# Splitting the weights of an fp32r encoder by two DMAs and a negation instead of a load, a cast and a subtraction

## The chip, the cores and the metric

The kernel runs on one core of one Trainium2 chip. The metric is the device time of one execution in microseconds, lower being better. The kernel before takes 1576.11 us (median of two runs, 1575.96 and 1576.26).

The core has five engines with a queue each, worked in order: TensorE (PE in the profile; PEld is its loading of the stationary operand), VectorE (DVE), ScalarE (ACT), GpSimd (POOL) and SyncE (SP). Transfers are started from a queue (SP or POOL here) and carried out by 16 DMA engines that all queues share.

## The reference

Two encoder layers over 512 positions of 1024 features, all in float32. Cut to the matrix products, which are nearly all of the work:

```
h = rmsnorm(x, g_mix[i]);  z = h @ w_in[i]              # 1024 -> 416 + 3*512 + 2*1024 columns
q = rmsnorm(c_q) @ w_uq[i];  kv = rmsnorm(c_kv) @ w_ukv[i]
...                                                     # per-head norm, rotary, softmax attention over 8 heads
y_conv = cb * dwconv(cc * cx, w_conv[i])
merged = g_a * (y_attn @ w_attn_up[i]) + g_c * (y_conv @ w_conv_up[i])
x = x + merged @ w_o[i]
u = dwconv(rmsnorm(x, g_ffn[i]) @ w_up[i], w_ffn_conv[i])   # 1024 -> 2 * 2816
x = x + (silu(a) * val) @ w_down[i]
x = x + sigmoid(rmsnorm(x, g_ple[i]) @ w_ple_gate[i]) * (p[i] @ w_ple[i])
```

## The kernel before

TensorE multiplies in float32r, a rounded form of float32. To keep precision each operand is held as two tiles: `h`, the operand rounded to float32r, and `lo`, the operand minus `h`. A product is then three matmuls (`mm3`, lines 88 to 90): h by h, h by lo and lo by h. A weight tile is 128 partitions by 1024 columns, 512 KB (416 KB for `w_a1`), and 250 of them go through the helper `weight` (line 78): 88 of `w_up`, 44 of `w_down`, 32 of `w_g`, 24 of `w_z`, 16 each of `w_o` and `w_pg`, 8 each of `w_au`, `w_cu` and `w_a1`, 4 of `w_ple` and 2 of `w_ukv`. `split` (line 92) does the same to activations, and to `w_uq` and `p`; it is not touched.

`weight` loads the tile from HBM into `raw` (three buffers) from SP's queue (line 80), casts it to `wh` on ACT (line 83) and subtracts on DVE to get `wl` (line 84). `wh` and `wl` have five buffers each. So up to three tiles can lie ready in `raw` while all five pairs are held by matmuls.

Two shapes of use matter. In `ws` (line 258) a weight is stationary: its 8 pieces by three matmuls, 24 in all, use it up before the next one (`w_z`, `w_g`, `w_up`; 4 pieces at a time for `w_au` and `w_cu`). In `proj` (line 511; `w_o`, `w_down`, `w_ple`, `w_pg`) the weights of one half of the output columns, four at a time with 8 input blocks, are all read again for each of the four blocks of 128 positions. They are therefore all held until the last block, and become free one after the other, shortly before those of the other half are wanted. This place is called a turn below.

A layer goes: latents with `w_a1`, heads, attention with the convolution's `w_z` products as filling work (here PE's order is written by hand), gates (`w_g`, `w_au`, `w_cu`), `w_o`, then three chunks of `w_up` and `w_down`, then `w_ple` and `w_pg`. Elsewhere a scheduler that simulates the kernel decides the order on every engine and which buffer a tile takes; a change of operations therefore also changes the order on PE. POOL does the small work of the norms (`rsqrt_eps`, lines 98 and 99) and of the rotary embedding (lines 242 to 253).

Of the kernel before, what the change touches and what calls it, by code (L numbers as in the profile page):

```python
# [11 lines left out]
F32 = mybir.dt.float32  # L12
# [3 lines left out]
AF = mybir.ActivationFunctionType  # L16
ALU = mybir.AluOpType
AX = mybir.AxisListType

P = 128  # L20
# [38 lines left out]
def encoder_kernel(ctx, tc, x_in, pT, pos, inv, w_a1, w_z, w_g, w_uq, w_ukv, w_au, w_cu, w_o,  # L59
                   w_up, w_down, w_pg, w_ple, b_gate, g_norm, g_lat, g_nope, g_rope, w_conv,  # L60
                   w_fconv, out):
    nc = tc.nc
    cp = ctx.enter_context(tc.tile_pool(name="cp", bufs=1))
    wp = ctx.enter_context(tc.tile_pool(name="wp", bufs=5))
# [11 lines left out]
        return ps.tile([P, S], F32, tag=tag, name="ps_" + tag, bufs={"mm": 2, "av": 1, "sc": 2, "tp": 3}[tag])  # L76

    def weight(src, n=1024):
        raw = wp.tile([P, n], F32, tag="raw", name="raw", bufs=3)
        nc.sync.dma_start(raw, src)  # L80
        h = wp.tile([P, n], F32R, tag="wh", name="wh")
        lo = wp.tile([P, n], F32R, tag="wl", name="wl")
        nc.scalar.copy(h, raw)  # L83
        nc.vector.tensor_sub(lo, raw, h.bitcast(F32))  # L84
        return h, lo

    def mm3(o, st, mv, start, stop):
# [100 lines left out]
    def layer(l, first):  # L188
        wa = []
        if first:  # L190
            nrm, close_nrm = pool("nrm", l)
            g1 = load_gain(l, 0, nrm)
            for i in range(4):
                wa.append(weight(w_a1[l, i], 2 * A1))
                if i < 3:
                    load_x(i + 1)
                norm(i, g1, nrm)
            close_nrm()
        else:
            wa = [weight(w_a1[l, i], 2 * A1) for i in range(4)]  # L200
# [6 lines left out]
        for i in range(2):  # L207
# [3 lines left out]
            split(w[0], w[1], raw)  # L211
            wu.append(w)
        wkv = weight(w_ukv[l])
        grope = mix.tile([P, 2, DR], F32, name="grope")
        nc.sync.dma_start(grope, g_rope[l:l + 1].broadcast_to([P, 2, DR]))
# [485 lines left out]
```

## Time and profile before

| | |
|---|---|
| median of the runs | 1576.11 us |
| span of the profiled execution | 1574.1 us |
| outside the span, against the median | 2.0 us |
| PE busy | 1557.1 us, 99% |
| DVE busy | 870.4 us, 55% |
| ACT busy | 684.4 us, 43% |
| POOL busy | 103.0 us, 7% |
| DMA from SP's queue | 140.90 MB, 27.2% of the 16 engines' time |
| granted TensorE clock, mean | 0.999 |

The profile is of one execution. Rows of operations give a line, an engine, the tile written and the tiles read, a count, the busy time in us and the mean in ns, and behind the bar the idle time of that engine just before, with what ended it. A busy time of PE is not PE at its peak, since matmuls overlap and their ends are modelled.

### The profile page before, as it was taken

How to read it: one execution, taken by the hardware profiler on the slowest of the kernel's cores; microseconds unless marked ns; L12 is line 12 of the kernel's file. 1: busy time of each engine (PE TensorE's matmuls, PEld its weight loads, DVE VectorE, ACT ScalarE, POOL GpSimd, SP SyncE). 2: the span in 40 equal slices, each digit the busy share in tenths (PEclk: the TensorE clock that was granted, in tenths of full speed). 3: DMA queues.
4: the chain of work that ended last, by engine and by line, in shares of the span. 5: the costliest groups of instructions: out<-in, count | busy, mean ns of one | idle time of the engine just before them, and what ended most of it. 6: DMA issues, size and time to landing. Idle time of an engine off the chain costs nothing.

```text
span 1574.1 us, 18521 instructions
## 1 busy us (share of the span) xinstructions
PE 1557.1 (99%) x7288; PEld 1280.1 (81%) x7288; DVE 870.4 (55%) x1228; ACT 684.4 (43%) x1088; POOL 103.0 (7%) x153
## 2 busy tenths in 40 slices
PE   7999999999999999999999999999999999999998
PEld 6888888888888888888888888888888888888886
DVE  7787553436544553555477775443565446535543
ACT  5678732325322431334464886222344234324342
POOL 2800000000000000001055000000000000000010
PEclk9999999999999999999999999999999999999999
DMA  6211122323213221323242102232232222232222
GB/s 205 93 55 41 54 94 94 106 69 129 95 61 130 93 95 58 132 96 94 71 133 81 41 28 92 81 107 81 85 118 94 94 94 94 80 107 94 94 68 79
DMA packets 41430, 142.06 MB, mean 90 GB/s; under 512 B 5761, under 2 KB 6273, under 8 KB 41345
## 3 DMA queue, kind: packets, MB, share of 16 engines
q1 hardware_dynamic: 41344, 140.90, 27.2%
q8 instruction: 57, 0.93, 0.2%
q14 instruction: 29, 0.23, 0.0%
HBM read 138.78 MB, written 2.10 MB: 90 GB/s over the span
## 4 chain that ended last, share of the span: by engine, by line
PE 94%; POOL 2%; DVE 2%; ACT 1%; DMA 1%; issue 1%; SPq 0%; DVEq 0%; POOLq 0%; ACTq 0%
PE ps_mm L89 14%; PE ps_mm L88 14%; PE ps_mm L90 14%; PE ps_sc L89 11%; PE ps_sc L88 11%; PE ps_sc L90 11%; PE ps_tp L89 4%; PE ps_tp L88 4%; PE ps_tp L90 4%; PE ps_tp L428 2%; PE ps_tp L125 1%; POOL rs L99 1%; PE ps_av L440 1%; PE ps_av L439 1%; PE ps_tp L394 1%; PE ps_av L88 1%
## 5 line engine op out<-in xcount | busy, mean ns | idle before, releaser
L84 DVE TENSOR_TENSOR wl<-raw,wh 128x1024 fp32r<-128x1024 f32 (+1 forms) x250 | 304.0, 1217 | 325.1 <-ACT wh L83 322.7
L83 ACT CAST wh<-raw 128x1024 fp32r<-128x1024 f32 (+1 forms) x250 | 260.8, 1046 | 425.6 <-PE ps_tp L90 120.3
L88 PE MATMUL ps_mm<-hh,wh 128*128 128x512 f32 (+1 forms) x832 | 326.4, 392 | 0.5 <-DVE ycv L355 0.5
L89 PE MATMUL ps_mm<-hl,wh 128*128 128x512 f32 (+1 forms) x832 | 322.9, 388 | 0.0
L90 PE MATMUL ps_mm<-hh,wl 128*128 128x512 f32 (+1 forms) x832 | 322.5, 388 | 0.0
L90 PEld LDWEIGHTS ps_mm<-hh,wl 128*128 128x128 f32 x832 | 156.6, 188 | 34.7
L88 PEld LDWEIGHTS ps_mm<-hh,wh 128*128 128x128 f32 x832 | 156.7, 188 | 33.2 <-DVE ycv L355 1.0
L89 PEld LDWEIGHTS ps_mm<-hl,wh 128*128 128x128 f32 x832 | 156.9, 189 | 32.5 <-DVE hl L94 0.4
L89 PE MATMUL ps_sc<-hl,wh 128*128 128x512 f32 (+1 forms) x368 | 142.2, 386 | 0.0
L90 PE MATMUL ps_sc<-hh,wl 128*128 128x512 f32 (+1 forms) x368 | 142.2, 386 | 0.0
L88 PE MATMUL ps_sc<-hh,wh 128*128 128x512 f32 (+1 forms) x368 | 142.1, 386 | 0.0
L98 POOL TENSOR_SCALAR ms<-ms 128x1 f32<-128x1 f32 (+2 forms) x40 | 15.8, 394 | 1389.0 <-ACT junk L117 1360.0
L89 PE MATMUL ps_tp<-wl,gth 128*128 128x512 f32 x256 | 100.6, 396 | 0.0
L90 PE MATMUL ps_tp<-wh,gtl 128*128 128x512 f32 x256 | 100.6, 395 | 0.0
L88 PE MATMUL ps_tp<-wh,gth 128*128 128x512 f32 x256 | 99.9, 395 | 0.0
L88 PEld LDWEIGHTS ps_sc<-hh,wh 128*128 128x128 f32 x368 | 69.3, 188 | 15.3
L90 PEld LDWEIGHTS ps_sc<-hh,wl 128*128 128x128 f32 x368 | 69.3, 188 | 15.3
L89 PEld LDWEIGHTS ps_sc<-hl,wh 128*128 128x128 f32 x368 | 69.3, 188 | 15.3
L93 ACT CAST gth<-fa 128x512 fp32r<-128x512 f32 x44 | 27.3, 620 | 120.1 <-DVE fa L574 120.1
L525 DVE TENSOR_TENSOR xs<-xs,ps_tp 128x512 f32<-128x512 f32 x32 | 21.6, 685 | 85.0 <-PE ps_tp L90 85.0
L572 ACT ACTIVATE fa<-fa 128x512 f32<-128x512 f32 x44 | 27.8, 632 | 88.5 <-DVE fa L547 88.5
L88 PEld LDWEIGHTS ps_tp<-wh,gth 128*128 128x128 f32 x256 | 48.1, 188 | 11.6
(242 smaller groups left out, 2671.2 us busy)
## 6 DMA issues: line engine op xcount, KB each, us to landing
raw<-in_w_up_dram SPq DMA_DIRECT2D x88, 512.0 KB, 3.5
raw<-in_w_down_dram SPq DMA_DIRECT2D x44, 512.0 KB, 3.4
raw<-in_w_g_dram SPq DMA_DIRECT2D x32, 512.0 KB, 3.5
raw<-in_w_z_dram SPq DMA_DIRECT2D x24, 512.0 KB, 3.5
raw<-in_w_o_dram SPq DMA_DIRECT2D x16, 512.0 KB, 3.5
raw<-in_w_pg_dram SPq DMA_DIRECT2D x16, 512.0 KB, 4.2
raw<-in_w_au_dram SPq DMA_DIRECT2D x8, 512.0 KB, 3.5
raw<-in_w_cu_dram SPq DMA_DIRECT2D x8, 512.0 KB, 3.5
```

The lines of the kernel that those rows point to most:

```text
L83: nc.scalar.copy(h, raw)
L84: nc.vector.tensor_sub(lo, raw, h.bitcast(F32))
L88: nc.tensor.matmul(o, st[0], mv[0], start=start, stop=False)
L89: nc.tensor.matmul(o, st[0], mv[1], start=False, stop=False)
L90: nc.tensor.matmul(o, st[1], mv[0], start=False, stop=stop)
L93: nc.scalar.copy(hi, src)
L98: nc.gpsimd.tensor_scalar_add(ms, ms, EPS)
L99: nc.gpsimd.tensor_tensor(r, ms, negh[:, :n], ALU.pow)
L125: nc.tensor.transpose(tp[:, j * P:(j + 1) * P], ht[:, j * P:(j + 1) * P], ident)
L428: nc.tensor.transpose(tp[:, k * P:(k + 1) * P], pe[:, k * P:(k + 1) * P], ident)
L525: nc.vector.tensor_tensor(xs[:, t, c], xs[:, t, c], o, ALU.add)
L572: nc.scalar.activation(a, a, AF.Silu)
```

## The change

`weight` no longer has a `raw` tile. A DMA from POOL's queue loads the tile straight into `wh`, converting to float32r on the way. ACT writes the negative of `wh` into `wl`. A second DMA from POOL's queue reads the same weights from HBM again and adds them into `wl`, which then holds the weight minus `wh`. Nothing else in the text is changed; the tiles `raw` of `w_uq` and `p` stay, and their loads stay on SP's queue.

```
     def weight(src, n=1024):
-        raw = wp.tile([P, n], F32, tag="raw", name="raw", bufs=3)
-        nc.sync.dma_start(raw, src)
         h = wp.tile([P, n], F32R, tag="wh", name="wh")
         lo = wp.tile([P, n], F32R, tag="wl", name="wl")
-        nc.scalar.copy(h, raw)
-        nc.vector.tensor_sub(lo, raw, h.bitcast(F32))
+        nc.gpsimd.dma_start(h, src)
+        nc.scalar.activation(lo, h.bitcast(F32), AF.Copy, scale=-1.0)
+        nc.gpsimd.dma_start(lo, src, accum_op=ALU.add)
         return h, lo
```

The scheduler makes a new order of this. Line numbers of the changed kernel are one lower from here on (its line 81 is the converting load, 82 the negation, 83 the adding DMA; 87 to 89 are the matmuls of `mm3`). Three places follow; the numbers in names only tell tiles of one program apart.

In the first run of `w_up` weights of the first layer, SP's queue had these loads in a row:

```order
L80 DMA raw_3672<-in_w_up_dram 128x1024
L80 DMA raw_3708<-in_w_up_dram 128x1024
L80 DMA raw_3748<-in_w_up_dram 128x1024
L80 DMA raw_3784<-in_w_up_dram 128x1024
L80 DMA raw_3822<-in_w_up_dram 128x1024
```

At that place POOL's queue now has loads (`wh`) and adding DMAs (`wl`, one number higher than its `wh`):

```order
L81 DMA wh_3650<-in_w_up_dram 128x1024
L83 DMA wl_3651<-in_w_up_dram 128x1024
L81 DMA wh_3689<-in_w_up_dram 128x1024
L81 DMA wh_3724<-in_w_up_dram 128x1024
L83 DMA wl_3690<-in_w_up_dram 128x1024
L83 DMA wl_3725<-in_w_up_dram 128x1024
L81 DMA wh_3761<-in_w_up_dram 128x1024
L83 DMA wl_3762<-in_w_up_dram 128x1024
L81 DMA wh_3796<-in_w_up_dram 128x1024
```

Nothing stood between the loads before. Now an adding DMA, which has to wait for the negation of its own `wh`, stands ahead of the next load: in turns behind one load and behind two.

At the turn of the first `w_down` chunk of the first layer (`wh_4102`, `wl_4103` and `wh_4108`, `wl_4109` are the first two weights of the other half, `gth` and `gtl` the split activation), PE's queue had:

```order
L88 MATMUL ps_tp_4124<-wh_4108,gth_3594 128x512
L88 MATMUL ps_tp_4150<-wh_4102,gth_3475 128x512
L89 MATMUL ps_tp_4150<-wl_4103,gth_3475 128x512
L90 MATMUL ps_tp_4150<-wh_4102,gtl_3476 128x512
L88 MATMUL ps_tp_4150<-wh_4102,gth_3475 128x512
L89 MATMUL ps_tp_4150<-wl_4103,gth_3475 128x512
L89 MATMUL ps_tp_4124<-wl_4109,gth_3594 128x512
L90 MATMUL ps_tp_4124<-wh_4108,gtl_3595 128x512
```

The same place now (`wh_4031` and `wh_4036` are the first two weights of the other half, `wh_4155` a weight of the next `w_up` run):

```order
L88 MATMUL ps_tp_4103<-wl_4032,gth_3423 128x512
L89 MATMUL ps_tp_4103<-wh_4031,gtl_3424 128x512
L87 MATMUL ps_tp_4103<-wh_4036,gth_3539 128x512
L87 MATMUL ps_mm_4160<-hh_71,wh_4155 128x512
L88 MATMUL ps_mm_4160<-hl_72,wh_4155 128x512
L88 MATMUL ps_tp_4051<-wl_4037,gth_3539 128x512
L89 MATMUL ps_tp_4051<-wh_4036,gtl_3540 128x512
```

The first matmul that needs the second weight's `lo` has moved back: 41 matmuls now stand between it and the last one that reads the buffer's old `wh`, where 30 stood before. Work of a third block of positions and of the next `w_up` run is put in between.

In the heads of the first layer POOL had these norms and rotary products in a row (`rs` is an inverse root, `ms` its argument):

```order
L98 TENSOR_SCALAR ms3_489<-ms3_489 128x3
L99 TENSOR_TENSOR rs3_493<-ms3_489,negh_74 128x3
L242 TENSOR_TENSOR sg_252<-sinT_82,grope_241 128x4x16 x4
L98 TENSOR_SCALAR ms24_549<-ms24_549 128x24
L251 TENSOR_TENSOR rb_510<-krope_261,sg_252 128x32
L99 TENSOR_TENSOR rs24_552<-ms24_549,negh_74 128x24
```

There it now has:

```order
L97 TENSOR_SCALAR ms3_484<-ms3_484 128x3
L83 DMA wl_624<-in_w_z_dram 128x1024
L98 TENSOR_TENSOR rs3_488<-ms3_484,negh_74 128x3
L83 DMA wl_720<-in_w_z_dram 128x1024
...
L97 TENSOR_SCALAR ms24_544<-ms24_544 128x24
L83 DMA wl_843<-in_w_z_dram 128x1024
L98 TENSOR_TENSOR rs24_547<-ms24_544,negh_74 128x24
L81 DMA wh_874<-in_w_z_dram 128x1024
```

The DMAs of the `w_z` weights have come in between the norms that the heads wait for.

## The prediction

> **What bounds the kernel now.** I read the page's busy times and chain first, then the costliest groups, then the waits, and last the timeline at a turn.
>
> ```profile
> span 1574.1 us, 18521 instructions
> PE 1557.1 (99%) x7288; PEld 1280.1 (81%) x7288; DVE 870.4 (55%) x1228; ACT 684.4 (43%) x1088; POOL 103.0 (7%) x153
> ...
> PE 94%; POOL 2%; DVE 2%; ACT 1%; DMA 1%; issue 1%; SPq 0%; DVEq 0%; POOLq 0%; ACTq 0%
> ```
>
> TensorE is the bound: it is busy 99% of the span and carries 94% of the chain that ended last. All that is not PE is 1574.1 - 1557.1 = 17 us, or 1.1%. No change that leaves the matmuls alone can gain 2%, and this one leaves them alone. The question is what it can lose.
>
> The pace of the matmuls is read from the timeline of PE in a `w_g` product:
>
> ```profile
> 300.42 0.39 PE L90 MATMUL ps_mm<-hh,wl 128*128 128x512 f32 x1
> 300.65 0.39 PE L88 MATMUL ps_mm<-hh,wh 128*128 128x512 f32 x1
> 300.88 0.40 PE L89 MATMUL ps_mm<-hl,wh 128*128 128x512 f32 x1
> 301.12 0.40 PE L90 MATMUL ps_mm<-hh,wl 128*128 128x512 f32 x1
> ```
>
> Three start in 0.70 us, so one takes 0.234 us, and the 24 of one weight tile 5.6 us. A new split tile has to be ready every 5.6 us wherever weights are streamed. How does it get ready?
>
> ```profile
> L84 DVE TENSOR_TENSOR wl<-raw,wh 128x1024 fp32r<-128x1024 f32 (+1 forms) x250 | 304.0, 1217 | 325.1 <-ACT wh L83 322.7
> L83 ACT CAST wh<-raw 128x1024 fp32r<-128x1024 f32 (+1 forms) x250 | 260.8, 1046 | 425.6 <-PE ps_tp L90 120.3
> ...
> raw<-in_w_up_dram SPq DMA_DIRECT2D x88, 512.0 KB, 3.5
> ```
>
> The view of waits shows what the cast waits for:
>
> ```profile
> ACT wh L83 <- PE ps_tp L90: 120.3, 24, 15.5
> ACT wh L83 <- PE ps_mm L89: 106.8, 65, 4.6
> ACT wh L83 <- PE ps_sc L89: 72.3, 56, 3.0
> ACT wh L83 <- PE ps_sc L90: 53.3, 20, 16.2
> ...
> ACT wh L83 <- DMA raw<-in_w_up_dram: 21.2, 11, 2.2
> ```
>
> In 24 + 65 + 56 + 20 = 165 of 250 cases the cast waited until a matmul gave its buffer back. The raw tile lay there already; the load waited for in the last row is the exception. So from release to ready there are now only a cast and a subtraction. ACT and DVE at the turn of the first `w_down` chunk:
>
> ```profile
> 469.41 1.05 ACT L83 CAST wh<-raw 128x1024 fp32r<-128x1024 f32 x1 [13.29 <-PE ps_tp L90]
> 470.81 1.05 ACT L83 CAST wh<-raw 128x1024 fp32r<-128x1024 f32 x1 [0.35 <-PE ps_tp L90]
> ```
> ```profile
> 470.50 1.23 DVE L84 TENSOR_TENSOR wl<-raw,wh 128x1024 fp32r<-128x1024 f32 x1 [1.80 <-ACT wh L83]
> ```
>
> Release at 469.4, ready at 470.50 + 1.23 = 471.7: 2.3 us.
>
> **What the change removes, adds and moves.** Off the path: 250 subtractions on DVE (304 us) go, and with 55% busy DVE isn't waited for in the stream, so this gains nothing. The 250 casts on ACT become 250 negations of the same shape: taken as 1.05 us each, no change. 250 issues leave SP, which nothing waits for. The `raw` tile goes, and with it the early load. That is what costs: after a release, two transfers in a row and a negation now stand where 2.3 us stood.
>
> Prices. The loads on SP's queue have
>
> ```profile
> q1 hardware_dynamic: 41344, 140.90, 27.2%
> ```
> ```profile
> L80 SPq DMA_DIRECT2D raw<-in_w_up_dram x88: 327/328/328, 333.2 to 1433.2; - x88
> ```
>
> 0.272 x 1574.1 = 428 us for 140.9 MB is 1.6 us of all 16 engines for a 0.524 MB tile. Landing at 3.5 us is then 0.33 of issue, 1.6 of transfer and 1.6 of tail. An issue from POOL isn't in this trace: between SP's 0.33 us and 1.2 us, the four-row product on POOL below; I take 0.7, in the middle. The adding transfer isn't either: it reads the weights and the tile and writes the tile. The ends are 1.6 us, if the second read costs nothing, and 4.8 if all three passes are in a row; I take 3.2, two reads in a row with the write beside them, since the engine that holds the sum needs both. A converting load I take at 1.6 like a plain one, and its upper end is in that range.
>
> The Trainium skill's DMA: Bandwidth & Descriptors (Anatomy of one DMA) fits transfers from GpSimd's queue as about 2.0 us plus bytes over 436e3; for this tile that is an estimate of 3.2 us, 1.2 of it transfer, against the 3.5 and 1.6 above. With 1.2 for both transfers of a tile the stream below would hide them, and the sum would lose its first term; but the fit is of plain loads, and no run here shows it from POOL.
>
> *The stream.* POOL works its queue in order. In the `w_up` run (first pair of order pieces) three tiles go as one load and its adding DMA, then two loads and their two. The engines move 3 x (1.6 + 3.2) = 14.4 us for them. But an adding DMA that stands right behind its own load can't be issued before the load has landed and is negated, and nothing is queued behind it: the engines idle for the tail 1.6, the negation 1.05 and the issue 0.7, 3.3 us. For two loads in a row the second transfer covers 1.6 of this, and 1.7 idle. Together 19.4 us for three tiles that PE uses up in 16.8: 0.87 us lost per tile. For 88 tiles of `w_up` and 48 of `w_g`, `w_au` and `w_cu` (with their runs taken like this one) that is 118 us. Up to 16.8 us the five buffers hide it all, so the term is 0 below an adding transfer of 2.3 us, and 2.5 us per tile at 4.8.
>
> *The turns.* From release to ready: issue 0.7, transfer and tail 3.2, negation 1.05, issue 0.7, transfer and tail 4.8: 10.5 us. What stands on PE between the old tile's last matmul and the first that needs the new `lo` is counted in the order, in full-width matmuls of 0.234 us: second `w_g` 36 (8.4 us), turns of two `w_down` chunks 41 (9.6), the `w_up` behind each of them 38 (8.9), `w_pg` 29 (6.8). Stalls 2.1 + 2 x 0.9 + 2 x 1.6 + 3.7 = 10.8 per layer, 21.6 for two. Third `w_up` tile of the second layer 32 (7.5): 3. `w_a1` between the layers 28 (6.5): 4. Sum 29 us. The ends: with 0.33 per issue and 1.6 for the adding transfer it takes 8.2 us and costs 6; with several tiles in the queue at a turn, or 1.2 and 4.8, some 80.
>
> *The heads.* From the chain of waits, and POOL's timeline for the sum of its products:
>
> ```profile
> 45.62 1.22 POOL sg L242 x4
> 46.84 0.08 issue
> 46.92 0.29 POOL ms L98
> 47.22 0.07 issue
> 47.29 0.26 POOL rb L251
> 47.54 4.15 POOL rs L99
> ```
>
> Here POOL itself is the chain, one piece after the other. Between these pieces now stand some eight DMAs of `w_z` (8 x 0.7 = 5.6 us), and where an adding DMA comes too early POOL stands still for its load, with the norm behind it: once, tail and negation, 2.7. That is 8 us per layer; at the start of the kernel the adding DMAs of `w_a1` stand behind the norms' roots and are read one after another, which I put at two adding transfers and a tail, 8 us. Sum 24, ends 4 and 50.
>
> Sum: 1574.1 + 118 + 29 + 24 = 1745, and with the 2.0 us outside the span 1747.
>
> **The rivals.** *The scheduler hides it all* (the other side, no slower). The adding transfer costs no more than a load, and an issue no more than SP's. Then the three tiles take 9.6 + 3.0 + 1.4 = 14.0 of 16.8 us, the turns cost 6, the heads 4: 1586 us. It decides from an adding transfer under 2.3 us together with a turn under 9 us. For it: the order was moved to give 41 matmuls for 30 at a turn, and DVE's lightened load. Against it: a second read has to come from somewhere.
>
> *Only the turns.* The adding transfer is near 2.2 us, the stream is hidden, and turns (up to 40) and heads (24) remain: 1576 + 64 = 1640.
>
> *The transfers themselves bound.* With 4.8 us the three tiles take 19.2 + 5.0 = 24.2, 2.5 us lost per tile on the 136 of the stream, 336; turns 80, heads 50: 2042; with 4.0 the stream loses 1.7 per tile, 227, and the sum with 60 and 40 is some 1900. For it: the share of the engines goes from 27.2% to four times that, over 100%, if all three passes count.
>
> *A slower TensorE after stalls.* At the start of the kernel, PE idles for 7.63 us and then works slowly:
>
> ```profile
> 7.63 1.97 PE L125 MATMUL ps_tp<-ident,ht 128*128 128x128 f32 x8 [7.63 <-DVE ht L122]
> ...
> 10.66 0.55 PE L88 MATMUL ps_mm<-wh,hh 128*128 128x416 f32 x1
> 11.01 0.55 PE L89 MATMUL ps_mm<-wl,hh 128*128 128x416 f32 x1
> ...
> 16.74 0.46 PE L89 MATMUL ps_mm<-wl,hh 128*128 128x416 f32 x1 [0.88 <-DVE wl L84]
> 17.03 0.35 PE L90 MATMUL ps_mm<-wh,hl 128*128 128x416 f32 x1
> 17.22 0.35 PE L88 MATMUL ps_mm<-wh,hh 128*128 128x416 f32 x1
> ```
>
> A matmul of 416 columns took 0.35 us there and 0.19 after; an idle time of 0.88 us didn't bring the slow pace back. Somewhere between 0.9 and 7.6 us is a length of stall that does. Six slow matmuls lose some 6 x 0.16 = 1.0 us, and if every stall of the stream (136 / 3 = 45, of 2.6 us) and of turns and heads (18) did it, 63 us come on top: 1810. For it stands that stalls of the right length are foreseen; against it that most are near 2.6 us or shorter. The Trainium skill's TensorE: Matmul & The Clock Gate (Part 1: The HAM clock gate) has the array at half clock after an idle window of about 3.4 us, until as long a busy one: the start agrees in kind, and by that rule the stalls of 2.6 us would stay free.
>
> *The change doesn't do what it says*: the load may keep all bits in `wh`, and `wl` would be zeros. No instruction's length hangs on the values here, so the time would be the same; it has no chance of its own.
>
> **How the numbers follow.** The forecast (1690 to 1800) 0.32, hidden 0.10, only the turns (1608 to 1690) 0.22, transfers as the bound (above 1840) 0.22, the slower TensorE (1800 to 1840) 0.13, faster 0.01. The time is that of the likeliest, 1747. The low end at 1615 leaves out the hidden case and little more, the high end at 1930 leaves out the upper half of the transfers' case: about 0.1 on each side. A measurement here can tell about 2%, 32 us, from no change: faster 0.01, the same 0.10, slower 0.89.
>
> **What would show each step.** In the profile after: the adding DMA's landing time against the load's (5 to 6 us against 4 if 3.2 holds); the DMA share in the `w_up` stretches near 3 x 28%, with ACT's negation ended by a DMA where the cast was ended by PE; PE waiting for `wh` or `wl` DMAs at L87 to L89, about 45 times 2.6 us in the stream and fewer, longer ones at `w_pg` and `w_a1`; POOL's queue as a releaser in the chain. If PE waits in the `w_up` stream are absent, the first term falls. If the DMA share is at its limit there, the third rival holds. What would make the whole wrong is an issue on POOL of several us, which appears in no row here, or ACT standing still for a load with PE's evictions behind its negation.

## The result and the profile after

The changed kernel takes 1798.95 us (median of two runs, 1798.93 and 1798.98) against 1576.11: a ratio of 1.1415, with a 95% interval of 1.1393 to 1.1437. It lost 223 us.

The page of the changed kernel gives the span, the busy time and share of each engine, the DMA queue of POOL (packets, MB, share of 16 engines' span) and the shares of the chain that ended last:

```profile
span 1796.8 us, 18546 instructions
PE 1632.8 (91%) x7288; PEld 1319.5 (73%) x7288; DVE 584.3 (33%) x978; ACT 682.9 (38%) x1088; POOL 447.5 (25%) x653
...
q0 software_dynamic: 72000, 260.60, 64.0%
...
issue 55%; PE 17%; POOL 15%; DMA 11%; ACT 2%; DVE 0%; POOLq 0%; SPq 0%; ACTq 0%
```
```profile
core 0: 1796.8 us, clock 0.956
```

The span is 222.7 us longer, and two numbers of PE make that up. It does the same 7288 matmuls, but is busy 1632.8 us where it was 1557.1: 75.7 us more. It is idle 1796.8 - 1632.8 = 164.0 us where it was 17.0: 147.0 more. So a third of the loss is longer busy time of PE, not waiting. Most of it is the clock: the mean granted clock is 0.956, where it was 0.999, and 120 us of PE's busy time lie in stretches with half the clock granted. At full clock they would have taken 60 us, so the clock accounts for an estimated 60 of the 75.7 us. The rest fits matmuls that no longer overlap next to a stall. (The chain, 94% PE before, now has most of its time in "issue", time in which an engine waited for nothing that the profile shows; it says little here. The waits say more.)

What PE waited for, in us, with the count and the longest one:

```profile
PE ps_tp L88 <- DMA wl<-in_w_down_dram: 47.3, 15, 6.4
PE ps_sc L89 <- DMA wl<-in_w_up_dram: 15.7, 4, 4.2
PE ps_mm L88 <- DMA wl<-in_w_o_dram: 14.1, 7, 3.1
PE ps_tp L124 <- DVE ht L121: 11.1, 3, 7.4
PE ps_mm L88 <- DMA wl<-in_w_down_dram: 11.0, 2, 6.3
PE ps_mm L88 <- DMA wl<-in_w_pg_dram: 10.9, 4, 4.2
PE ps_sc L89 <- DMA wl<-in_w_cu_dram: 9.5, 4, 4.1
PE ps_mm L88 <- DMA wl<-in_w_a_dram: 7.6, 3, 4.9
PE ps_mm L87 <- DMA wh<-in_w_up_dram: 5.8, 4, 1.5
...
PE ps_mm L89 <- DMA wl<-in_w_g_dram: 4.9, 4, 2.2
```

By weight: `w_down` 47.3 + 11.0 = 58.3, `w_up` 15.7 + 5.8 + 0.5 (a smaller row) = 22.0, `w_o` 14.1, `w_pg` 10.9, `w_cu` 9.5, `w_a1` 7.6, `w_g` 4.9. It is nearly always the `wl` of the adding DMA, seldom the `wh` of the load.

Behind it stand the waits of the other engines, from the same view, and the new operations in the costliest groups and the DMA issues (the last figure is us from issue to landing):

```profile
POOL wl L83 <- ACT wl L82: 774.2, 208, 8.8
...
ACT wl L82 <- DMA wh<-in_w_up_dram: 236.8, 68, 23.8
```
```profile
L82 ACT ACTIVATE wl<-wh 128x1024 fp32r<-128x1024 f32 (+1 forms) x250 | 263.7, 1055 | 743.4 <-DMA wh<-in_w_up_dram 236.8
...
L83 POOL DMA_DIRECT2D wl<-in_w_up_dram x88 | 77.2, 877 | 315.0 <-ACT wl L82 267.1
...
L81 POOL DMA_DIRECT2D wh<-in_w_up_dram x88 | 59.8, 696 | 141.1 <-PE ps_tp L89 77.7
...
wh<-in_w_up_dram POOLq DMA_DIRECT2D x88, 512.0 KB, 6.0
wl<-in_w_up_dram POOLq DMA_DIRECT2D x88, 512.0 KB, 5.6
```

In 208 of 250 cases POOL stood at an adding DMA until the negation was done, and nothing behind it in POOL's queue could start. The negation on ACT, whose forerunner waited for PE to release a buffer, now waits for the load.

POOL's timeline at the end of the first `w_up` run and the start of `w_down` (start, duration, line, count; in brackets the idle time before and its releaser):

```profile
466.40 1.39 POOL L81 DMA_DIRECT2D wh<-in_w_up_dram  x2
474.24 0.88 POOL L83 DMA_DIRECT2D wl<-in_w_up_dram  x1 [6.44 <-ACT wl L82]
475.78 0.88 POOL L83 DMA_DIRECT2D wl<-in_w_up_dram  x1 [0.66 <-ACT wl L82]
476.34 0.89 POOL L81 DMA_DIRECT2D wh<-in_w_up_dram  x1
485.20 0.85 POOL L83 DMA_DIRECT2D wl<-in_w_up_dram  x1 [7.98 <-ACT wl L82]
485.81 1.36 POOL L81 DMA_DIRECT2D wh<-in_w_down_dram  x2
```

Two loads, their two adding DMAs, one load, its adding DMA, and again: three tiles from 466.40 to 485.81, 19.4 us. The rounds of three tiles before and after it, from 445.97 and to 506.12, take 20.4 and 20.3. The stretches by engine busy time, clock and DMA share show who pays:

```profile
466.40:485.81 19.41, 19.36 (x83) 15.28 (x82) 5.81 (x9) 6.69 (x9) 4.33 (x8) 1.00 0.71 163
485.81:506.12 20.31, 14.18 (x58) 10.38 (x56) 7.26 (x11) 6.66 (x9) 4.28 (x7) 1.00 0.68 155
```

In the first PE (the first busy time) works without a gap, on tiles that were ready earlier. In the second it does not; the DMA engines are used to 0.7 in both. The waits of PE there:

```profile
498.94 0.50 PE L88 MATMUL ps_tp<-wl,gth 128*128 128x512 f32 x1 [2.40 <-DMA wl<-in_w_down_dram]
...
510.92 0.79 PE L88 MATMUL ps_tp<-wl,gth 128*128 128x512 f32 x1 [6.36 <-DMA wl<-in_w_down_dram]
```

A `w_down` tile gets six matmuls here before the next one is wanted (two input blocks by three), 1.4 us; in `w_up` it got 24. Four tiles are wanted in 5.6 us, and POOL delivers three in 20. What the `w_up` run had drawn from the buffers is paid here. Over the whole trace, 50 of the 58.3 us of waits for `w_down` lie at such an entry and 8.3 at the turns. The 22.0 us for `w_up` all lie in the first two tiles of the run that comes with and behind a turn of `w_down`; later in a `w_up` run PE doesn't wait.

### The profile page after: what moved, and what is told of

It is laid out like the page before. It is cut to its first block, busy times and chain, and to the rows that moved or that the text cites. A ratio compares the mean times of both kernels' runs of the same rounds, so it can differ in the third digit from the quotient of the medians.

```text
span 1796.8 us, 18546 instructions
## 1 busy us (share of the span) xinstructions
PE 1632.8 (91%) x7288; PEld 1319.5 (73%) x7288; DVE 584.3 (33%) x978; ACT 682.9 (38%) x1088; POOL 447.5 (25%) x653
## 4 chain that ended last, share of the span: by engine, by line
issue 55%; PE 17%; POOL 15%; DMA 11%; ACT 2%; DVE 0%; POOLq 0%; SPq 0%; ACTq 0%
POOL wl L83 8%; POOL wh L81 6%; PE ps_mm L88 3%; PE ps_mm L89 3%; PE ps_mm L87 2%; PE ps_sc L89 2%; PE ps_sc L88 2%; PE ps_sc L87 2%; DMA wh<-in_w_up_dram 2%; DMA wl<-in_w_pg_dram 1%; ACT wl L82 1%; DMA wh<-in_w_o_dram 1%; DMA wl<-in_w_a_dram 1%; DMA wl<-in_w_o_dram 1%; PE ps_tp L88 1%
## 5 line engine op out<-in xcount | busy, mean ns | idle before, releaser
L82 ACT ACTIVATE wl<-wh 128x1024 fp32r<-128x1024 f32 (+1 forms) x250 | 263.7, 1055 | 743.4 <-DMA wh<-in_w_up_dram 236.8
L87 PE MATMUL ps_mm<-hh,wh 128*128 128x512 f32 (+1 forms) x832 | 330.2, 397 | 9.7 <-DMA wh<-in_w_up_dram 5.8
L89 PE MATMUL ps_sc<-hh,wl 128*128 128x512 f32 (+1 forms) x368 | 145.9, 397 | 15.8 <-DMA wl<-in_w_up_dram 15.7
L83 POOL DMA_DIRECT2D wl<-in_w_up_dram x88 | 77.2, 877 | 315.0 <-ACT wl L82 267.1
L88 PE MATMUL ps_tp<-wl,gth 128*128 128x512 f32 x256 | 108.4, 429 | 47.3 <-DMA wl<-in_w_down_dram 47.3
L545 DVE SCALAR_TENSOR_TENSOR fa<-ps_sc,wfc,fa 128x511 f32<-128x511 f32 x44 | 33.0, 750 | 243.5 <-ACT fa L544 243.5
L89 PE MATMUL ps_tp<-wh,gtl 128*128 128x512 f32 x256 | 105.9, 420 | 0.0
L87 PE MATMUL ps_tp<-wh,gth 128*128 128x512 f32 x256 | 104.9, 422 | 0.0
L88 PEld LDWEIGHTS ps_tp<-wl,gth 128*128 128x128 f32 x256 | 52.0, 203 | 66.6 <-DMA wl<-in_w_down_dram 54.5
L81 POOL DMA_DIRECT2D wh<-in_w_up_dram x88 | 59.8, 696 | 141.1 <-PE ps_tp L89 77.7
L83 POOL DMA_DIRECT2D wl<-in_w_down_dram x44 | 38.6, 877 | 162.2 <-ACT wl L82 162.2
```

What stands on the lines that cost most here:

```text
L81: nc.gpsimd.dma_start(h, src)
L82: nc.scalar.activation(lo, h.bitcast(F32), AF.Copy, scale=-1.0)
L83: nc.gpsimd.dma_start(lo, src, accum_op=ALU.add)
L87: nc.tensor.matmul(o, st[0], mv[0], start=start, stop=False)
L88: nc.tensor.matmul(o, st[0], mv[1], start=False, stop=False)
L89: nc.tensor.matmul(o, st[1], mv[0], start=False, stop=stop)
```

## The experiments

All compare with the kernel before on the same chip, 1575.8 to 1576.4 us. Where no interval is given, the time is of a single execution; repeated ones of one kernel lay within 0.5%. PE idle is the span less PE's busy time. The diffs of the last four are against the kernel before, the others against the changed kernel.

| kernel | time us | PE busy | PE idle | clock |
|---|---|---|---|---|
| before | 1576.11 | 1557.1 | 17.0 | 0.999 |
| after | 1798.95 | 1632.8 | 164.0 | 0.956 |
| own pairs | 2015.12 | 1708.0 | 305.0 | 0.937 |
| loads ahead | 1724.21 | 1618.7 | 103.5 | 0.969 |
| six buffers | 1724.29 | 1602.3 | 120.1 | 0.966 |
| ahead and six | 1654.03 | 1581.5 | 76.4 | 0.989 |
| no add | 1640.47 | 1582.4 | 55.9 | 0.990 |
| ahead, no add | 1623.22 | 1577.8 | 43.4 | 0.994 |
| add only | 1672.84 | 1595.0 | 76.1 | 0.979 |
| cast only | 1593.43 | 1561.9 | 29.7 | 0.998 |
| projections as before | 1667.41 | 1587.3 | 78.3 | 0.989 |
| projections alone | 1652.55 | 1579.7 | 71.1 | 0.991 |

**The theory**: POOL's queue, in order, holds the next load back behind an adding DMA that waits for its own load and negation. **The rival**: the order costs nothing; it is only the longer way from a released buffer to a ready tile that PE sees.

*Own pairs.* In the loop over the chunks of `w_up` and `w_down`, POOL's order is the one written in the code: each load, then its adding DMA. It takes the scheduler's freedom to put two loads together.

```
+        pool_order = tc.manual_schedule(engines={mybir.EngineType.Pool})
+        pool_order.__enter__()
...
+        pool_order.__exit__(None, None, None)
```

> The changed kernel with POOL's order in the chunks of w_up and w_down fixed to the order of the text: every adding DMA right behind its own load (126 tiles in both layers). Theory POOL's order (an adding DMA that waits behind its own load keeps the next load from starting, and the DMA engines idle): per tile 1.4 us of load, 2.6 us of adding and 3.6 us idle, 7.6 us against 5.6 on PE, so the chunks take about 126 x 7.6 = 958 us against some 830 now: about 1925 us. Theory latency (what counts is only the 13 us from a buffer's release to its new tile, whatever stands between on POOL): as the changed kernel, about 1800 us.

2015.12 us, 216 more than the change and 90 more than the theory expected. The operations, transfers and buffers are the same, in another order on POOL; the rival expected no such thing. PE's idle time is 305.0 us, 141 more, and the other 75 us are PE's busy time, which the expectation had not counted. PE's order is not quite the same either: it differs in `w_down`'s chunks and just behind them. In the `w_up` runs it is all but the same, and the waits for `w_up` rise from 22.0 to 125 us:

```profile
PE ps_mm L89 <- DMA wl<-in_w_up_dram: 64.3, 32, 3.1
PE ps_sc L89 <- DMA wl<-in_w_up_dram: 61.0, 36, 3.0
```

*Loads ahead.* In the same loop, the other way round: `ahead` lists the sources of a chunk's tiles in their order of use, and `take`, called in place of `weight`, always issues the load and negation of the next tile ahead of the adding DMA of the one it returns.

```
+    def begin(src):
+        h = wp.tile([P, 1024], F32R, tag="wh", name="wh")
+        lo = wp.tile([P, 1024], F32R, tag="wl", name="wl")
+        nc.gpsimd.dma_start(h, src)
+        nc.scalar.activation(lo, h.bitcast(F32), AF.Copy, scale=-1.0)
+        return h, lo
+    def take():
+        while ahead and sum(len(x) == 3 for x in ahead) < 2 and any(len(x) == 1 for x in ahead):
+            i = next(i for i, x in enumerate(ahead) if len(x) == 1)
+            ahead[i] = (*begin(ahead[i][0]), ahead[i][0])
+        h, lo, src = ahead.pop(0)
+        nc.gpsimd.dma_start(lo, src, accum_op=ALU.add)
+        return h, lo
```

> The changed kernel with POOL's order in the same chunks fixed the other way: the load of the next tile always stands ahead of the adding DMA of this one. Theory POOL's order: the engines have the next load to do while a tile is negated, 4.0 us per tile and no idle time that counts, so the stalls at the entry into w_down and in the w_up runs go and those at the turns stay: about 1740 us. Theory latency: release to ready is no shorter, about 1800 us. Theory engines (the transfers' own time decides): about 1800 us too.

1724.21 us, 75 less than the change and 291 less than the pairs. POOL's timeline in a `w_up` run (its line 91 is the load, 100 the adding DMA):

```profile
569.54 0.55 POOL L91 DMA_DIRECT2D wh<-in_w_up_dram  x1 [2.00 <-PE ps_mm L106]
571.66 0.86 POOL L100 DMA_DIRECT2D wl<-in_w_up_dram  x1 [1.57 <-ACT wl L92]
575.16 0.55 POOL L91 DMA_DIRECT2D wh<-in_w_up_dram  x1 [2.63 <-PE ps_sc L106]
577.11 0.88 POOL L100 DMA_DIRECT2D wl<-in_w_up_dram  x1 [1.40 <-ACT wl L92]
```

A load goes out every 5.6 us, PE's own pace, and waits for PE to release a buffer: the stream is hidden. PE's wait for `w_down` falls accordingly:

```profile
PE ps_tp L105 <- DMA wl<-in_w_down_dram: 11.6, 5, 3.5
PE ps_mm L106 <- DMA wl<-in_w_up_dram: 11.0, 4, 3.7
```

Where 58.3 us stood (47.3 + 11.0), 11.6 are left. The theory holds for this region, though here too the scheduler moved some matmuls of `w_down`'s chunks. Most other regions keep their waits (`w_o` 13.3, `w_cu` 10.8 by the same view); `w_pg` alone fell, from 10.9 to 1.3, which the theory does not explain.

*Six buffers.* Latency alone should be cured by one more pair of buffers. The memory comes from `raw`, which is no longer used by `weight`.

```
-    wp = ctx.enter_context(tc.tile_pool(name="wp", bufs=5))
+    wp = ctx.enter_context(tc.tile_pool(name="wp", bufs=6))
...
-        raw = wp.tile([P, 1024], F32, tag="raw", name="raw", bufs=3)
+        raw = wp.tile([P, 1024], F32, tag="raw", name="raw", bufs=1)
```

> The changed kernel with six instead of five buffers each for wh and wl (and one instead of three for the few remaining raw tiles, to make room). Theory latency: a tile more of lead, up to 5.6 us, at nearly every place against stalls of 2 to 6.6 us, so most stalls go: about 1630 us. Theory POOL's order: the pace of the queue stays and a run's debt is smaller by one tile's lead only, the turns gain: about 1720 us.

1724.29: the value of the theory, not of the rival. PE's waits in `w_down` are still there, while none for `w_up` is in its list any more:

```profile
PE ps_tp L88 <- DMA wl<-in_w_down_dram: 40.8, 13, 6.3
```

One more buffer lengthens the credit; it doesn't shorten POOL's cycle.

*Ahead and six.* Both together.

> POOL's next load issued ahead of each adding DMA in the chunk loops, and six weight buffers in place of five (each alone gave 1724). If the two cure different places (the order the w_down runs, 61 us of w_down's own time, the sixth buffer the entry of the w_up runs and w_g, some 30 us), they add up: 1724 - 40 = about 1680, and what stays lies at w_o, w_pg, w_a1, w_cu and the attention, which the order does not reach. If one bottleneck (a transfer pair that is simply too long for the stream) is behind both, the second cure adds little: 1715.

1654.03 us, ratio to before 1.0492 (1.0475 to 1.0510). The gains of 75 and 75 add up to 145 of 150: they cure different places. The 40 us expected of the second cure were too few: the step from 1724 to 1654 is 70 us. Between the two profiles (this one is of the slowest of four executions, 1659.65) PE's busy time alone falls by 37 us (1618.7 to 1581.5), which the expectation had not counted. What remains is mainly `w_o`, `w_pg` and the first norm of the kernel:

```profile
PE ps_mm L105 <- DMA wl<-in_w_o_dram: 15.9, 5, 5.6
PE ps_tp L141 <- DVE ht L138: 12.4, 1, 12.4
PE ps_mm L105 <- DMA wl<-in_w_pg_dram: 9.5, 6, 3.4
```

Neither edit alone shortens the waits for `w_o` (13.3 and 14.5 us). Each alone had shortened those for `w_pg` (to 1.3 and 4.2), so its 9.5 with both is not explained.

*No add.* A plain converting load in place of the adding DMA, into the same tile, behind the same wait.

```
-        nc.gpsimd.dma_start(lo, src, accum_op=ALU.add)
+        nc.gpsimd.dma_start(lo, src)
```

> The changed kernel with the adding DMA replaced by a second converting load into the same tile, so the weight minus its rounded part is left out (wl holds the weight). This prices the second read. All theories expect its 4 KB packets at about 174 ns instead of 327. POOL's order: three tiles take 8.4 us of transfers and 5.8 idle, 14.2 of 16.8, so the runs lose nothing and only turns stay: about 1710. Latency: 56 stalls shorter by 1.2 us each and fewer slow matmuls after them, about 1710. Engines: nothing left over the kernel before but a little, about 1620.

1640.47 us: 158 of the 223 us hang on the second transfer being an adding one. This is the cleanest of the comparisons, for the orders of PE and of POOL's DMAs are those of the changed kernel; so the new order by itself, beside plain loads, costs at most the 64 us that are left. The theory and its rival both expected about 1710 and missed by 70; nearest was 1620, the value if the transfers' own time decides. The theory had kept the turns at their old cost, but they became cheap too: PE waits 2.2 us for `w_down`, 1.5 for `w_pg` and 1.4 for `w_o`. The page of this kernel, of the one with the adding DMA alone and of the one with the converting load alone give the price of each kind of transfer, as MB and share of 16 engines' span (lines in this order):

```profile
q0 software_dynamic: 72000, 260.60, 51.1%
```
```profile
q0 software_dynamic: 36000, 130.30, 44.2%
```
```profile
q0 software_dynamic: 36000, 130.30, 26.3%
```

130.30 MB are 248.5 tiles of 0.524 MB. In spans of 1638.3, 1671.1 and 1591.6 us a converting load takes 837 / 497 = 1.68 us of all engines (1.68 also in the third), an adding transfer 739 / 248.5 = 2.97. (The 1.4 and 2.6 us in the expectations come from the median packet of 4 KB, 174 and 327 ns, eight to an engine and tile.)

*Ahead, no add.* The plain load in the order of "loads ahead".

> The same order on POOL, and a plain converting load in place of the adding DMA; the subtraction is left out. The plain load alone gave 1640, the order alone 1724. If the rest of 64 us at 1640 is POOL's order too, this falls to about 1605. If it is the longer way from release to ready, and the heads, which the order does not touch, it stays at 1635 to 1645.

1623.22 us, ratio 1.0302 (1.0286 to 1.0317): between the two values, so both have a part. (The orders of PE and POOL are those of "loads ahead".) Of the 64 us that stay when the adding is gone, POOL's order in this loop is worth 17; for 47 it is not needed.

*Add only.* The load into `raw` and the cast stay; DVE negates, POOL adds.

```
         nc.sync.dma_start(raw, src)
...
         nc.scalar.copy(h, raw)
-        nc.vector.tensor_sub(lo, raw, h.bitcast(F32))
+        nc.vector.tensor_scalar_mul(lo, h.bitcast(F32), -1.0)
+        nc.gpsimd.dma_start(lo, src, accum_op=ALU.add)
```

> The kernel before with the adding DMA alone: raw loaded early on SP's queue and cast on ACT as before, the negative made on DVE, and POOL's DMA adds the weights. POOL's queue then holds adding DMAs without loads behind them, and from a release to a ready tile it takes a cast, a negation, an issue and one transfer, about 8 us instead of 13. Theory POOL's order: nothing to hold up, and the loads are early again: 1580 to 1610 us. Theory engines (1.4 + 2.6 us of transfers for every tile, as in the changed kernel): as slow as the changed kernel, 1750 to 1800 us.

1672.84 us, 97 over before; both expected values were missed. On POOL nothing but the next adding DMA and the small work of the norms stands behind one that waits, so the theory expected little. But the adding transfer still lies between release and use, and the loads beside it land later:

```profile
raw<-in_w_up_dram SPq DMA_DIRECT2D x88, 512.0 KB, 7.5
wl<-in_w_up_dram POOLq DMA_DIRECT2D x88, 512.0 KB, 7.4
```

The load landed in 3.5 us before. PE waits at the turns: `w_pg` 16.3, `w_up` 13.8 us.

*Cast only.* The converting load into `wh` by POOL; `raw` by SP and the subtraction on DVE as before.

```
-        nc.scalar.copy(h, raw)
+        nc.gpsimd.dma_start(h, src)
```

> The kernel before with the converting load alone: wh is loaded by POOL's queue with conversion, raw by SP's queue as before (two loads of 1.4 us per tile), DVE subtracts. From a release to a ready tile: an issue, a load and a subtraction, 6 to 7 us. Theory POOL's order: no adding DMA stands ahead of a load: 1580 to 1610 us. If the landing of a load from POOL's queue itself were the cost (6.0 us at the median in the changed kernel), most of the loss would be here already: above 1680 us.

1593.43 us, 17 over before, as expected. Taking the cast off ACT (684.4 to 444.6 us busy) gains nothing that shows, and a second read of all weights costs little by itself. The two halves cost 97 + 17 = 114; together they cost 223. The other 109 appear only with both on one queue, one waiting for the other, without the early load into `raw`; the runs do not part these.

*Projections.* The old helper for `w_o`, `w_down`, `w_ple` and `w_pg` (80 tiles) and the new for the rest; then the reverse.

```
-                wt = [weight(ws_[n * (KTOT // 2) + k // 2]) for k in ks if k % 2 == 0]
+                wt = [weight_was(ws_[n * (KTOT // 2) + k // 2]) for k in ks if k % 2 == 0]
```

> The changed kernel with the old helper for the weights of w_o, w_down, w_ple and w_pg (80 tiles, all those with turns), the new one for the other 170. Forecast's terms, with the measured adding time: the stream's term stays, turns go, about 1700 us. Theory POOL's order: the debt of a w_up run is paid where tiles are wanted in quick succession, at w_down's entry, and there the tiles now come another way: about 1640 us.

> The kernel before with the new helper for the weights of w_o, w_down, w_ple and w_pg alone (80 tiles). By the forecast's terms only turns cost here, 29 us: about 1605 us. Theory POOL's order: at each turn three or four tiles are wanted within 5 us and come at the queue's pace of 6 to 8 us each or in a burst, some 8 us a turn and cold matmuls after: about 1690 us.

1667.41 and 1652.55 us: 91 and 77 over before, 168 together, again less than 223. Neither time is at one of the expected values; both lie between. Either half of the weights loses when it is split this way; 55 us need both. The waits for `w_down` show the debt of the `w_up` runs being paid there: with `w_down` split the new way and `w_up` the old way ("projections alone") they are 17.7 us and 2.1 in a smaller row, against 58.3 with both:

```profile
PE ps_tp L97 <- DMA wl<-in_w_down_dram: 17.7, 10, 3.9
```

## Why the prediction was right, and where not

**The time.** 1747 us, a range of 1615 to 1930 and "slower" at 0.89 were forecast; 1798.95 is 52 above the point and inside the range. The sum was of idle time only: 171 us. PE's idle time grew by 147.0, 24 less than that, and PE's busy time by 75.7, for which the sum had nothing. The point came near because errors cancel in part: the stream was put too high, the turns too low, and the clock left out. That is luck.

**What bounds.** Right. DVE's busy time fell from 870.4 to 584.3 us, and no gain shows; only the way of the weights counted.

**Prices.** POOL's issue: 0.7 taken, 0.70 and 0.88 measured. Negation: 1.05 taken, 1.055. Converting load: 1.6, measured 1.68. Adding transfer: 3.2 (two reads in a row, the write beside them), measured 2.97. The pair is 4.8 against 0.640 x 1796.8 / 497 tiles x 2 = 4.63 in the changed kernel itself. That the adding transfer is two reads in a row is not shown by this. The adding DMA lands 5.6 us after its issue, as foreseen; the load 6.0 instead of 4. With no adding transfers beside it the load lands in 4.5 ("no add").

The fit of the Trainium skill's DMA: Bandwidth & Descriptors (Anatomy of one DMA), which the prediction set beside this, made an estimate of 3.2 us for such a transfer, 1.2 of them data. No group of 512 KB from POOL was that quick here: the lowest median is 3.8 us (`w_cu`, with the converting load alone).

**The stream.** The mechanism and its period were right: 19.4 us per three tiles, measured 20.4, 19.4 and 20.3 against 16.8 of PE. The step that failed is the multiplication: "For 88 tiles of `w_up` and 48 of `w_g`, `w_au` and `w_cu` (with their runs taken like this one) that is 118 us." It took each lost microsecond of POOL for a stall of PE. Inside the `w_up` runs PE doesn't wait: they work off the five buffers. The debt falls due at the entry of `w_down`, where a tile is worth 1.4 us of matmuls at first: 50 us. With `w_cu`'s 9.5 the term is some 60 us, half of what it was put at. Two runs show that it is one debt: `w_down`'s waits of 58.3 us become 11.6 with "loads ahead", and 19.8 when only `w_up`'s tiles come the old way.

**The turns.** This term was too small: 29 us were forecast, and 65 measured. By place, forecast first: second `w_g` 4.2 and 4.9; turns of `w_down` 3.6 and 8.3; `w_up` behind them 6.4 and 22.0; `w_pg` 7.4 and 10.9; `w_a1` between the layers 4 and 4.9; a third `w_up` tile 3 and nothing; `w_o`, which was left out, 14.1. One reason shows in the medians: from release to ready it is not 10.5 us but 6.0 + 1.06 + 5.6 = 12.7, since the load lands later. The prediction knew of several tiles in the queue (the end of 80) but took the value for one.

**The heads.** 24 were forecast. PE's waits on ACT and DVE, for `w_z` and for `w_a1` at the start were about 33 us, some 12 of which were there before: 21. The size is right by luck, for the places are not. At the start of the kernel PE waits 6 us longer, where 8 were foreseen; in the heads and the attention of both layers 4 to 5, where 16 were; the other 11 us lie behind the norms after `w_o` and `w_pg` and at `w_ple`, where none were.

**The TensorE clock.** This is what the point lacked. The prediction priced it as a rival at 63 us and gave it 0.13, believing that the stalls of 2.6 us were too short. They are not. The stall of 2.04 us before 108.74 is followed by slow matmuls, the longer one of 3.18 us before 1203.18 is not (PE's timeline of the changed kernel; between the two, stretches of 3.41 us, with the granted clock before the last two numbers):

```profile
108.74 0.66 PE L427 MATMUL ps_tp<-ident,pe 128*128 128x128 f32 x4 [2.04 <-ACT pe L415]
...
109.60 0.63 PE L88 MATMUL ps_mm<-hl,wh 128*128 128x512 f32 x1
110.03 0.63 PE L89 MATMUL ps_mm<-hh,wl 128*128 128x512 f32 x1
```
```profile
105.88:109.29 3.41, 1.37 (x9) 0.89 (x8) 0.86 (x2) 2.94 (x6) 0.88 (x1) 1.00 0.77 121
109.29:112.70 3.41, 3.41 (x12) 2.75 (x12) 2.13 (x5) 2.82 (x6) 0.00 (x0) 0.50 1.01 177
1198.14:1201.56 3.42, 1.86 (x8) 1.15 (x7) 0.00 (x0) 0.87 (x1) 0.00 (x0) 1.00 1.06 244
1201.56:1204.97 3.41, 1.79 (x8) 1.49 (x9) 0.00 (x0) 1.31 (x3) 0.89 (x1) 1.00 0.99 244
```
```profile
1203.18 0.50 PE L89 MATMUL ps_sc<-yc,wl 128*128 128x512 f32 x1 [3.18 <-DMA wl<-in_w_cu_dram]
1203.52 0.40 PE L87 MATMUL ps_sc<-yc,wh 128*128 128x512 f32 x1
1203.75 0.39 PE L88 MATMUL ps_sc<-yc,wh 128*128 128x512 f32 x1
```

Start to start a matmul takes 0.43 us after the first and 0.23 after the second. The clock changes only at the ends of such stretches, which lie on one grid over the whole trace. The first stall lies whole in one stretch, which is idle for 2.04 us, and the next has half the clock. The second is divided, 1.56 and 1.62 us, and the clock stays full in both and in the stretch behind them. So what decides is the idle time within one stretch; the last section has the count. The rule that the prediction leaned on (the Trainium skill, TensorE: Matmul & The Clock Gate, Part 1: half clock after an idle window of about 3.4 us) agrees in the length of the window, but the window need not be idle throughout.

**The rivals.** *Hidden* was to decide "from an adding transfer under 2.3 us together with a turn under 9 us". With a second transfer of 1.68 us and no adding at all the time was 1640, not 1586, so this was out of reach. *Only the turns* gave 1640 for a cheap second transfer. That is the time of "no add", but by luck: its sum was 64 us of idle time, and PE's idle time there grew by 38.9 and its busy time by 25.3. *The transfers bound* falls: the engines are used to 0.7 in the stretches above, and the same transfers took 1654 us in another order with one more buffer. *Slower TensorE* (1810) came true together with the forecast, not instead of it. Its 63 us are near the 60 that the clock cost, but in another way: 28 stretches at half clock cost some 2.1 us each, where 63 stalls at 1.0 were priced.

**What would make it wrong** did not happen: POOL's issue took 1.25 us at most, and PE's waits for ACT (its `hh`, `pe` and `pw` rows) are 5.1 + 3.9 + 3.0 = 12 us in all.

What stays open: how the 16 us at `w_o`, the 9.5 at `w_pg` and the 12 us before the first norm's product (the `ht` row; 7.6 in the kernel before) in "ahead and six" come about. With a plain load PE waits 1.4 us for the `wl` of `w_o` ("no add"), so the adding transfer is in it; another order of POOL there was not tried. No version beat the kernel before, in which PE idles for 17 us.

## What to carry over

An operation that is taken off an engine with time to spare gains nothing, and a DMA that waits for a computation stops every DMA behind it on its queue: count the period of such a queue (transfers, plus the tail, the computation and the issue that nothing covers) and compare it with the pace of the consumer. If it is longer, buffers only move the bill to the place where tiles are wanted fastest; issuing the next independent load ahead of the waiting DMA shortens it (here 2015 us at the worst order, 1799 as scheduled, 1724 with loads ahead). When the consumer is TensorE, price a stall of about 2 us or more with the longer busy time behind it as well: here 0.5 us for each us of added idle time (75.7 on 147.0), and 0.4 to 0.8 in the other kernels.

## What the runs showed of the hardware

- TensorE went to half clock after stalls shorter than the prediction expected. In the traces of the twelve kernels, of stalls that stand alone (no other over 0.6 us in the 15 us before or the 6 us behind), 6 of 83 between 0.6 and 1.9 us were followed by half clock within 6 us, 30 of 41 between 1.9 and 3.0 us, 13 of 16 between 3.0 and 3.5, and all 25 longer ones. The granted clock changes in windows of 3.41 us on one fixed grid, and the idle time within one window sorts the cases. In the eleven traces of changed kernels, from the first record of the clock on (14 to 33 us into the span), all 168 windows at full clock in which PE idled for 1.9 us or more were followed by half clock. Of the 4964 with less, 15 were; all of these had over 1.6 us.
- An adding DMA costs 2.97 us of all engines for 0.524 MB where a converting load costs 1.68: 1.8 times. Single packets of 4 KB show nearly the same ratio, 327 ns (median) against 174.
- In the changed kernel the issue of a converting load occupies POOL for 0.53 to 0.97 us and that of an adding DMA for 0.85 to 1.25 (0.70 and 0.88 on average for `w_up`). 500 of them bring POOL from 103.0 to 447.5 us of busy time, which by itself was never the bound (25%).
